# First three hgrn projections taken two chunks of K at a time with the first conditions; norms and transposes ahead of the conditions

## The chip, the cores and the metric

The kernel runs on one core of a Trainium2 chip. The metric is the device time of one execution in microseconds (us); lower is better. The engines are TensorE (PE, with its weight loads shown as PEld), VectorE (DVE), ScalarE (ACT), GpSimd (POOL) and SyncE (SP, which issues the DMAs). All times on rows count from the start of the profiled span.

## The reference

The reference is two transformer blocks in float32 on 256 latent tokens and, in the first block's first layer, 256 context tokens, with width 1024. What matters here is the very beginning of the first block:

```python
m_lat = (silu(c) @ ada_w[0] + ada_b[0])[:, None]        # and the same with c_ctx
sh1, sc1, g1, sh2, sc2, g2 = split(m_lat, 6)
h_lat = rmsnorm(x, norm_g[0, 0]) * (1.0 + sc1) + sh1     # and the same for ctx
z = h @ ab_w_in[0]            # columns: pool 512 | q 512 | zf 512 | zb 512 | v 512 | g 512
q = silu(q); f = lb + (1 - lb) * sigmoid(z_dir); k = 1 - f   # zf forward, zb backward
# gated scan over the tokens for four heads of 128, both directions, then
# output norm, gate, output projection, feed-forward layers, the second layer, the second block
```

`lb` comes from a softmax over `hg_lower`. The first scale `sc1` and shift `sh1` (here: the conditions) need 2 x 1024 columns of `ada_w`, which is 8 MB, before any product with `h` can be made.

## The kernel before

A Python tracer writes the instructions down; a planner in the library then decides each engine's order from the program order and from when operands would be ready, and buffers with the same tag take turns in a fixed number of slots (`bufs`). `issue_after(e)` makes what is traced inside it on e's engine come behind `e` on that engine.

Every large product is split in three: each float32 operand becomes `hi` (ACT, L149) and `lo` (DVE, L150), and `mm3` (L172) makes three matmuls hi·hi, hi·lo and lo·hi into one PSUM tile. A piece of weights goes by DMA into `raw` (four buffers of 512 KB, L161) and is split from there. PSUM has eight banks: three with the tag A, two B, two tr and one C.

The prologue stands in `block1` (L1574) and its helpers. Token tiles 2 and 3 are the context, 0 and 1 the latent. `setup` loads `c` and `c_ctx` and makes `cvec`; the four tiles of x come in; then `ada_first` (L571) returns `step` and `columns`. `step(g)`, g = 0 to 3, loads four buffers `adaw` of 512 KB (L589), multiplies them with `cvec` (sixteen matmuls for each of scale and shift, counted as the profile counts them, L591), adds the bias by one more (L592) and copies the result to `first` (DVE, L595). `columns(g)` turns two chunks of 128 features into columns (L602) and writes `sc` and `sh` (L603 to L605). `modulate(g)` makes h for the same two chunks, scaled and shifted and split into `xh` and `xl`.

The order in the program is: `step(0)`; `gains()`, which loads six small sets of rows by SP's queue (L298) and transposes them; then for each stream its two tiles through `normed` (L642: two Squares on ACT, a power on POOL by L268, scaling on DVE and ACT; its result `u` lives in `big`, two buffers) and sixteen transposes (L237) with copies back over x (L1608); then for g = 1 to 5 the `step(g)`, `columns(g-1)`, `modulate(g-1)` and `products(g-2)`. `products` makes only the first of the three projections of the first two heads, q, two chunks of K at a time: twelve matmuls of 512 columns. The other two, zf and zb, are made in `hgrn_mixer` (L696), `project(0)`, parts 1 and 2, each over all eight chunks at once; part 2 does the context stream first, as 96 matmuls of 256 columns. Behind each part stand a sigmoid (ACT, L745), F and B on DVE (L751, L752) and a product with q on POOL (L759).

Then `levels` (L762) builds the scan in seven levels, a chain over POOL, ACT, PE and DVE (L767 to L807). Beside it PE has two projections of 512 columns for all four tiles (`kept` and `gated`, L866 and L867, 96 matmuls of 512 columns each) and the matmuls of further conditions (`fill`, L529, eight at a time). `outputs(0)` follows (L823 to L848), then `project(1)` and so on.

Of the kernel before, what the change touches and what calls it, by code (L numbers as in the profile page):

```python
# [17 lines left out]
P = 128  # L18
D = 1024
# [62 lines left out]
class Kern:  # L82
# [89 lines left out]
    def mm3(self, ps, lh, ll, rh, rl, first, last):  # L172
        for i, (l, r) in enumerate(((lh, rh), (lh, rl), (ll, rh))):
            self.T.matmul(ps, l, r, start=first and i == 0, stop=last and i == 2)  # L174
            next(self.aside, None)

# [57 lines left out]
    def transposes(self, ps, src, blocks):  # L234

        for i, b in enumerate(blocks):
            self.T.transpose(ps[:, i], src[:, b * P:(b + 1) * P], self.ident)  # L237
# [7 lines left out]

    def new_xT(self):
        self.place = 1 - self.place
        return self.xh[:, self.place], self.xl[:, self.place]
# [42 lines left out]
    def columns(self, rows, name, pool=None):  # L291
# [211 lines left out]
    def gains(self):  # L503
# [8 lines left out]
            (d["pool_scale"].rearrange("o (g p) -> (o g) p", p=P), 4)], "colsA")  # L512
# [58 lines left out]
    def ada_first(self):  # L571
# [5 lines left out]
        every = self.t(self.aw, [P, 2], "every")  # L577
        V.reduce_sum(every, self.ident.rearrange("p (j n) -> p n j", n=32)[:, 0:2], axis=AX.X)
        bias = self.t(self.aw, [24, 256], "bias")
        self.dma(bias, self.d["ada_b"][0].rearrange("(p n) -> p n", p=24))  # L580
        rows = {}

        def step(g):
            ps = self.ps((P, 2, 256))
            for v in (1, 0):

                for h in range(2):
                    raw = self.t(self.aw, [P, 1024], "adaw", bufs=4).rearrange("p (k n) -> p k n", k=4)
                    self.dma(raw, w[:, 4 * h:4 * h + 4, v * 1024 + g * 256:v * 1024 + g * 256 + 256])  # L589
                    for j in range(4):  # L590
                        T.matmul(ps[32 * j:32 * j + 32, v], self.cvec[:, 4 * h + j], raw[:, j], start=h == 0, stop=h == 1 and j != 0)  # L591
                end = T.matmul(ps[0:32, v], self.ident[:24, 4 * v + g:4 * v + g + 1].to_broadcast([24, 32]), bias,  # L592
                               start=False, stop=True)
            rows[g] = self.t(self.aw, [P, 2, 256], "first", bufs=1)
            return end.ins, V.tensor_copy(rows[g], ps).ins  # L595

        def columns(g):
            k = slice(2 * g, 2 * g + 2)
            pc = self.ps((P, 2, 2, 2), "C")
            for v in (1, 0):  # L600
                for c in range(2):
                    T.matmul(pc[:, v, c], rows[g][:, v, c * P:(c + 1) * P], every, start=True, stop=True)  # L602
# [4 lines left out]
        return step, columns, sc, sh  # L607
# [34 lines left out]
    def normed(self, x):  # L642
# [9 lines left out]
        S.activation(u[:, 512:D], x[:, 512:D], AF.Copy, scale=r)  # L652
# [43 lines left out]
    def hgrn_mixer(self, xT, q0, fill):  # L696
# [3 lines left out]
        with self.scope("hg") as hp:  # L700

            mx = self.t(hp, [P, 8], "lbm")
            V.tensor_max(mx, self.hgl[:, 0], self.hgl[:, 1])
            e = self.t(hp, [P, 2, 8], "lbe")
# [1121 lines left out]
```

## Time and profile before

| | us |
|---|---|
| median of 3 runs | 2154.99 (2154.59 to 2156.27) |
| the profiled execution, its own time | 2158.11 |
| its span in the trace | 2156.3 |
| PE busy in the span | 2093.5 (97%) |

The span is what the rows cover; 1.8 us of the profiled execution's time lie outside it, and it is 3.1 us above the median. A busy PE is not always a PE at its peak: a matmul counts from its start to the modelled end, and those in a row overlap. So the pace of PE is read from the starts of its matmuls and from the granted clock.

### The profile page before, as it was taken

Reading aid. Unit: us, or ns where it says so; the run is one execution under the profiler, and the core shown is the slowest. Engines: PE = TensorE matmul, PEld = TensorE weight load, DVE = VectorE, ACT = ScalarE, POOL = GpSimd, SP = SyncE. Lnnn points to the kernel's source line nnn. Section 1 sums busy time; section 2 is a strip of 40 time slices with the busy share of each in tenths; the row PEclk is TensorE's granted clock in tenths of the full one; section 3 lists DMA queues with packets and bytes.
Section 4 is the critical chain, followed back from the end, with each engine's and each line's share of the span. In section 5 each row is a group of like instructions: output and inputs, shape, how many; then the busy total and the mean of one; then the engine's idle time right before and its main releaser. Section 6 shows DMA issues by size and latency. Waiting matters only on the chain. (4 is left out here: it accounts for less than half of the span.)

```text
span 2156.3 us, 33891 instructions
## 1 busy us (share of the span) xinstructions
PE 2093.5 (97%) x13178; PEld 1819.7 (84%) x13178; DVE 1365.8 (63%) x2496; ACT 970.5 (45%) x1904; POOL 160.0 (7%) x182
## 2 busy tenths in 40 slices
PE   7999999999999889999999989999999999999998
PEld 4787878787887668998998878998899889889987
DVE  4656658856535887554754677554855498876556
ACT  4232444322324555543644485543644265355443
POOL 0423200000000210000000000000000012110000
PEclk9999999999999999999999999999999999999999
DMA  9632327767432414655766527655666465137653
GB/s 318 209 125 79 108 74 238 226 207 232 137 102 65 144 38 150 204 181 171 219 180 187 179 75 220 205 181 175 190 205 183 156 167 148 50 110 226 189 184 104
DMA packets 238941, 352.58 MB, mean 164 GB/s; under 512 B 14432, under 2 KB 185020, under 8 KB 238652
## 3 DMA queue, kind: packets, MB, share of 16 engines
q1 hardware_dynamic: 238780, 350.41, 52.2%
q8 instruction: 104, 1.70, 0.3%
q14 instruction: 57, 0.47, 0.1%
HBM read 349.31 MB, written 1.05 MB: 162 GB/s over the span
## 5 line engine op out<-in xcount | busy, mean ns | idle before, releaser
L150 DVE TENSOR_TENSOR lo<-raw,hi 128x512 fp32r<-128x512 f32 (+1 forms) x1072 | 696.3, 692 | 381.2 <-ACT hi L149 379.8
L149 ACT ACTIVATE hi<-raw 128x512 fp32r<-128x512 f32 (+1 forms) x1072 | 601.9, 617 | 740.1 <-issue 356.6
L174 PE MATMUL B<-xh,hi 128*128 128x256 f32 (+1 forms) x1200 | 366.8, 306 | 1.6 <-ACT r L1137 1.4
L174 PE MATMUL B<-xl,hi 128*128 128x256 f32 (+1 forms) x1200 | 366.2, 305 | 1.0 <-DVE xl L150 1.0
L174 PE MATMUL B<-xh,lo 128*128 128x256 f32 (+1 forms) x1200 | 366.6, 306 | 0.0
L174 PE MATMUL A<-xh,hi 128*128 128x256 f32 (+1 forms) x1008 | 304.6, 302 | 0.4 <-ACT a L1383 0.2
L174 PE MATMUL A<-xh,lo 128*128 128x256 f32 (+1 forms) x1008 | 303.5, 302 | 0.7 <-DVE lo L150 0.7
L174 PE MATMUL A<-xl,hi 128*128 128x256 f32 (+1 forms) x1008 | 303.6, 301 | 0.0
L174 PEld LDWEIGHTS B<-xh,hi 128*128 128x128 f32 x1200 | 229.5, 191 | 12.1 <-ACT r L1137 1.6
L174 PEld LDWEIGHTS B<-xl,hi 128*128 128x128 f32 x1200 | 229.6, 191 | 11.3 <-DVE xl L150 1.9
L174 PEld LDWEIGHTS B<-xh,lo 128*128 128x128 f32 x1200 | 229.6, 191 | 10.2 <-issue 1.2
L174 PEld LDWEIGHTS A<-xh,hi 128*128 128x128 f32 x1008 | 193.5, 192 | 8.9 <-ACT hi L149 2.0
L174 PEld LDWEIGHTS A<-xh,lo 128*128 128x128 f32 x1008 | 193.5, 192 | 8.4 <-DVE lo L150 2.0
L174 PEld LDWEIGHTS A<-xl,hi 128*128 128x128 f32 x1008 | 193.6, 192 | 6.1
L174 PE MATMUL B<-hi,xh 128*128 128x512 f32 (+1 forms) x464 | 169.0, 365 | 3.0 <-ACT v L974 1.6
L174 PE MATMUL B<-lo,xh 128*128 128x512 f32 (+1 forms) x464 | 166.9, 360 | 0.0
L174 PE MATMUL B<-hi,xl 128*128 128x512 f32 (+1 forms) x464 | 166.5, 360 | 0.0
L268 POOL TENSOR_TENSOR pow<-rv,mhalf 128x1 f32<-128x1 f32 (+2 forms) x54 | 42.8, 793 | 1441.6 <-DVE rv L273 744.6
L174 PE MATMUL B<-hi,hl 128*128 128x512 f32 x308 | 122.1, 396 | 0.0
L174 PE MATMUL A<-lo,hh 128*128 128x512 f32 x308 | 121.9, 396 | 0.1
L174 PE MATMUL A<-hi,hl 128*128 128x512 f32 x308 | 121.9, 396 | 0.0
L174 PE MATMUL A<-hi,hh 128*128 128x512 f32 x308 | 121.8, 395 | 0.0
(438 smaller groups left out, 3267.5 us busy)
## 6 DMA issues: line engine op xcount, KB each, us to landing
adaw<-in_ada_w SPq DMA_DIRECT2D x96, 512.0 KB, 4.8
raw<-in_ffn_wg SPq DMA_DIRECT2D x88, 512.0 KB, 4.7
raw<-in_ffn_wu SPq DMA_DIRECT2D x88, 512.0 KB, 4.7
raw<-in_ffn_wd SPq DMA_DIRECT2D x88, 512.0 KB, 4.1
raw<-in_ffn_w_in SPq DMA_DIRECT2D x88, 256.0 KB, 4.2
raw<-in_ffn_w_in SPq DMA_DIRECT2D x44, 512.0 KB, 4.5
raw<-in_ab_w_in SPq DMA_DIRECT2D x38, 512.0 KB, 4.6
raw<-in_ffn_w_out SPq DMA_DIRECT2D x38, 512.0 KB, 4.6
```

The source lines that it names most:

```text
L149: self.S.activation(hi, src, AF.Copy)
L150: self.V.tensor_tensor(lo, src, hi.bitcast(F32), op=ALU.subtract)
L174: self.T.matmul(ps, l, r, start=first and i == 0, stop=last and i == 2)
L268: self.G.tensor_tensor(r, x, exponent_tile[:, :x.shape[1]], op=ALU.pow)
```

## The change

It touches only what runs up to the end of the first two heads' projections, and the loads behind them.

- `gains()` and the bias of the conditions are loaded by ACT's queue instead of SP's.
- A new function `first_products` holds the prologue. The adaw loads are issued ahead of the steps, in two sets of four buffers that take turns; the weights of all three projections are loaded and split in halves of K into tiles of their own (48 KB a partition).
- All norms and transposes come first. Every later block of PE's work is chained behind the one before it by `issue_after`: `step(g)`, the q product of group g-1, `columns(g)`, `modulate(g)`, the zf and zb products of group g-1. Last come all three products of group 3. So the six PSUM tiles of the three projections are open at once (two B, three A, one tr), and the steps share one bank of tr.
- `hgrn_mixer` gets the three finished projections; `project(0)` only does what stands behind them. The softmax for `lb` moves to `forget()`, its Exp behind the last norm on ACT.
- The splits of `kept`'s weights on ACT come behind the last sigmoid of `project(0)`.

```diff
@@ gains, columns
-                self.dma(t[at:at + r, :], ap)
+                (dma or self.dma)(t[at:at + r, :], ap)
...
+            (d["pool_scale"].rearrange("o (g p) -> (o g) p", p=P), 4)], "colsA", dma=self.nc.scalar.dma_start)
@@ ada_first
-        self.dma(bias, self.d["ada_b"][0].rearrange("(p n) -> p n", p=24))
-        rows = {}
+        self.nc.scalar.dma_start(bias, self.d["ada_b"][0].rearrange("(p n) -> p n", p=24))
+        ps = self.pst((P, 2, 256))
+        rows, raws = {}, {}
+
+        def load(g):
+            for v in (1, 0):
+                for h in range(2):
+                    raw = self.t(pool if g % 2 else self.aw, [P, 1024], "adaw", bufs=4).rearrange("p (k n) -> p k n", k=4)
+                    raws[g, v, h] = raw
+                    self.dma(raw, w[:, 4 * h:4 * h + 4, v * 1024 + g * 256:v * 1024 + g * 256 + 256])
@@ hgrn_mixer
-                    given = pr == part == 0
-                    if not given:
+                    if pr:
                         wh, wl = self.piece([P, 8, 256], lambda r: [(r, wv[:, :, c0 + 512 * part:c0 + 512 * part + 256])])
...
-                    ps = q0 if given else [self.ps((P, 2, 256), "B") for _ in range(2)]
+                    ps = [self.ps((P, 2, 256), "B") for _ in range(2)] if pr else given[part]
...
-                            for kc in range(0 if given else 8):
+                            for kc in range(8 if pr else 0):
...
-            self.tok_major(self.tiles_of(xT), order, self.wcols(w, 2048, 512), 512, kept, "B")
+            with self.tc.issue_after(hg0_end):
+                pcs = self.wcols(w, 2048, 512)
+            self.tok_major(self.tiles_of(xT), order, pcs, 512, kept, "B")
@@ new
+    def first_products(self, pool, xs):
...
+        load, step, columns, sc, sh = self.ada_first(pool)
+        wv = self.d["ab_w_in"][0].rearrange("(k p) f -> p k f", p=P)
+        w = [[self.t(pool, [P, 8, 256], f"{n}{i}", F32R) for n in ("hi", "lo")] for i in range(3)]
+
+        def weights(h):
+            own = slice(4 * h, 4 * h + 4)
+            for i, (hi, lo) in enumerate(w):
+                raw = self.t(self.w, [P, 4, 256], "raw", bufs=2 * self.nraw)
+                self.dma(raw, wv[:, own, 512 + 512 * i:768 + 512 * i])
+                for k in (0, 2):
+                    self.split(hi[:, 4 * h + k:4 * h + k + 2], lo[:, 4 * h + k:4 * h + k + 2], raw[:, k:k + 2])
+
+        load(0)
+        self.gains()
+
+        for s in (1, 0):
+            uu = [self.normed(xs[2 * s + t]) for t in range(2)]
+            for t, u in enumerate(uu):
+                for c0 in range(0, 8, 4):
+                    ps = self.pst((P, 4, P))
+                    end = self.transposes(ps, u, range(c0, c0 + 4))
...
+        with self.tc.issue_after(self.last):
+            self.lb = self.forget()
...
+        acc = [[self.ps((P, 2, 256), tag) for tag in tags] for tags in ("BB", "AA", ("A", "tr"))]
+
+        def products(g, parts):
+            for i in parts:
+                hi, lo = w[i]
+                for h in range(2):
+                    cut = slice(h * P, (h + 1) * P)
+                    for k in (2 * g, 2 * g + 1):
+                        end = self.mm3(acc[i][h], hi[:, k, cut], lo[:, k, cut], self.xh[:, :, k], self.xl[:, :, k], k == 0, k == 7)
+            return end
...
+        for g in range(4):
+            if g == 0:
+                weights(0)
+                load(1)
+            elif g < 3:
+                load(g + 1)
+            if g == 1:
+                weights(1)
+            for f in (lambda: step(g), lambda: g and products(g - 1, (0,)), lambda: columns(g),
+                      lambda: modulate(g), lambda: g and products(g - 1, (1, 2))):
+                with self.tc.issue_after(end):
+                    end = f() or end
+        with self.tc.issue_after(end):
+            end = products(3, range(3))
+        return acc
```

## Rows read from the trace of the kernel before

**Rows 1.** The page: busy time, share of the span and instructions by engine.

```profile
PE 2093.5 (97%) x13178; PEld 1819.7 (84%) x13178; DVE 1365.8 (63%) x2496; ACT 970.5 (45%) x1904; POOL 160.0 (7%) x182
```

**Rows 2.** Windows: stretch, length, busy by engine (instructions), granted clock, DMA share, GB/s.

```profile
20.10:33.00 12.90, 11.17 (x101) 5.42 (x100) 9.13 (x24) 7.41 (x16) 1.10 (x2) 1.00 0.95 325
33.00:37.50 4.50, 4.50 (x18) 3.67 (x17) 3.50 (x10) 1.75 (x4) 0.00 (x0) 0.64 1.03 332
37.50:54.00 16.50, 15.24 (x94) 10.04 (x92) 9.33 (x22) 8.99 (x16) 0.00 (x0) 1.00 1.07 342
54.00:76.60 22.60, 22.60 (x144) 20.42 (x145) 12.13 (x19) 6.84 (x14) 5.89 (x4) 1.00 0.46 142
76.60:88.00 11.40, 9.69 (x78) 7.37 (x77) 8.97 (x11) 4.90 (x8) 7.46 (x7) 0.85 0.77 241
88.00:150.00 62.00, 61.77 (x357) 47.49 (x356) 33.57 (x55) 17.33 (x30) 21.70 (x30) 1.00 0.47 151
```

**Rows 3.** Timeline, PE and DVE, first condition: start, length, engine, line, tiles, count [idle].

```profile
10.73 1.08 PE L591 MATMUL A<-adaw,cvec 128*32 128x256 f32 x8 [6.02 <-DMA adaw<-in_ada_w]
...
13.98 1.94 PE L591 MATMUL A<-adaw,cvec 128*32 128x256 f32 x16
...
16.84 0.34 PE L301 MATMUL tr<-ident,rows 52*128 52x52 f32 x1
16.94 0.69 DVE L595 COPY first<-A 128x512 f32<-128x512 f32 x1 [7.35 <-PE A L592]
```

**Rows 4.** Timeline, ACT, Silu and norms of the first two tiles.

```profile
4.00 0.31 ACT L496 ACTIVATE rows<-rows 16x128 f32<-16x128 f32 x1
...
5.25 0.63 ACT L649 ACTIVATE big<-r 128x512 f32<-128x512 f32 x1 [0.94 <-DMA r<-in_ctx]
...
9.11 0.72 ACT L652 ACTIVATE big<-r,pow 128x512 f32<-128x512 f32 x1 [0.49 <-POOL pow L268]
```

**Rows 5.** Tile rows: issues by line, duration ns min/median/max, first and last start.

```profile
L298 SPq DMA_DIRECT2D rows<-in_norm_g x4: 287/296/1920, 7.4 to 10.1; - x4
```

**Rows 6.** Timeline, PE: transposes early and later.

```profile
17.11 3.08 PE L237 MATMUL tr<-ident,big 128*128 128x128 f32 x12
...
26.41 0.63 PE L237 MATMUL tr<-ident,big 128*128 128x128 f32 x4 [0.73 <-DVE big L651]
```

**Rows 7.** Timeline, PE: last condition, columns, and the products behind them.

```profile
38.62 1.07 PE L591 MATMUL A<-adaw,cvec 128*32 128x256 f32 x16
...
41.71 1.05 PE L602 MATMUL C<-every,first 128*128 128x2 f32 x8
...
42.63 0.48 PE L174 MATMUL B<-xh,hi 128*128 128x512 f32 x1
```

**Rows 8.** Timeline: from the first columns to the first product.

```profile
28.57 0.95 PE L602 MATMUL C<-every,first 128*128 128x2 f32 x8
...
34.10 0.65 PE L174 MATMUL B<-xh,hi 128*128 128x512 f32 x1
```

**Rows 9.** Timeline, all engines, where the projections end.

```profile
71.13 0.38 ACT L745 ACTIVATE sg<-B 128x256 f32<-128x256 f32 x1 [1.42 <-PE B L174]
...
72.62 1.40 POOL L759 TENSOR_TENSOR A<-q,F 128x512 f32<-128x512 f32 x1 [2.68 <-DVE F L751]
...
76.61 1.05 PE L772 MATMUL A<-q,ks 128*128 128x128 f32 x8
...
77.60 1.93 PE L529 MATMUL C<-adaw,cvec 128*32 128x256 f32 x32
...
79.81 3.60 DVE L150 TENSOR_TENSOR lo<-raw,hi 128x512 fp32r<-128x512 f32 x3
...
81.67 1.77 PE L772 MATMUL A<-q,ks 128*128 128x128 f32 x8 [1.71 <-POOL ks L767]
```

**Rows 10.** Timeline: last step of the levels, first transpose of the outputs.

```profile
117.44 0.18 DVE L807 TENSOR_TENSOR F<-F 128x8 f32<-128x8 f32 x1
...
150.33 0.60 PE L823 MATMUL tr<-ident,B 128*128 128x128 f32 x4
```

More of the change, by code (lines that the diff above doesn't have):

```diff
@@ L173, in mm3 @@
         for i, (l, r) in enumerate(((lh, rh), (lh, rl), (ll, rh))):
-            self.T.matmul(ps, l, r, start=first and i == 0, stop=last and i == 2)
+            m = self.T.matmul(ps, l, r, start=first and i == 0, stop=last and i == 2)
             next(self.aside, None)
+        return m.ins
     @contextlib.contextmanager
@@ L289, in bcast, with columns @@
         return t
-    def columns(self, rows, name, pool=None):
+    def columns(self, rows, name, pool=None, dma=None):
         n = sum(r for _, r in rows)
@@ L601, in columns @@
                 for c in range(2):
-                    T.matmul(pc[:, v, c], rows[g][:, v, c * P:(c + 1) * P], every, start=True, stop=True)
+                    end = T.matmul(pc[:, v, c], rows[g][:, v, c * P:(c + 1) * P], every, start=True, stop=True)
             V.tensor_scalar(sc[:, k], pc[:, 1], 1.0, 32.0, op0=ALU.add, op1=ALU.mult)
@@ L605, in columns @@
             V.tensor_copy(sh[:, k], pc[:, 0])
-        return step, columns, sc, sh
+            return end.ins
+        return load, step, columns, sc, sh
     def ada_cols(self, l, v):
@@ L693, in post_end, with hgrn_mixer @@
             self.V.scalar_tensor_tensor(out[:, sl], self.post_y[tl, h], r, x[:, sl], op0=ALU.mult, op1=ALU.add)
[L696 removed]
+    def hgrn_mixer(self, xT, given, fill):
         d, V, S, G, T = self.d, self.V, self.S, self.G, self.T
@@ L1595, in block1 @@
                 self.dma(xs[tl], xin[tl])
-            step, columns, sc, sh = self.ada_first()
-            step(0)
-            self.gains()
-            wv = d["ab_w_in"][0].rearrange("(k p) f -> p k f", p=P)
-            for s in (1, 0):
-                uu = [self.normed(xs[2 * s + t]) for t in range(2)]
-                for t, u in enumerate(uu):
-                    for c0 in range(0, 8, 4):
-                        ps = self.pst((P, 4, P))
-                        self.transposes(ps, u, range(c0, c0 + 4))
-                        self.V.tensor_copy(xs[2 * s + c0 // 4].rearrange("p (c n) -> p c n", n=256)[:, :, t * P:(t + 1) * P], ps)
@@ L1631, in block1 @@
-            for g in range(1, 6):
-                with contextlib.ExitStack() as after:
-                    if g < 4:
-                        for e in step(g):
-                            after.enter_context(self.tc.issue_after(e))
-                    if g < 5:
-                        columns(g - 1)
-                        modulate(g - 1)
-                    if g == 1:
-                        piece = self.piece([P, 8, 256], lambda r: [(r, wv[:, :, 512:768])])
-                    if g > 1:
-                        products(g - 2)
@@ L1643, in block1 @@
-            cat = self.hgrn_mixer(xT, q0, self.ada(0, (2, 4, 3)))
+            with self.scope("start") as start:
+                given = self.first_products(start, xs)
+            xT = [self.halves(i) for i in range(2)]
+            cat = self.hgrn_mixer(xT, given, self.ada(0, (2, 4, 3)))
             first.close()
```

91 lines of the change are left out of this document (47 added, 44 removed).

## The prediction

> **What bounds the kernel now.** I read the page first: PE is busy for 2093.5 us of the span, far more than any other engine [rows 1]. So a gain is either less work on PE or less of its time lost. The change leaves PE's work as it is: the same step, column, transpose and product matmuls, in another order. It can only win back time that PE loses in the stretch it touches. Second I read the windows of that stretch, to see where PE is short of its pace [rows 2]. From 54.0 to 76.6 it is busy all the time, with 144 matmuls for the last two projections (48 of 512 columns, 96 of half that): 22.6 us, 11.3 a projection. So 2.8 us is the price of one projection's two chunks, and 8.5 of all three. Ahead of that PE sits idle 1.7 us between 20.1 and 33, 1.3 between 37.5 and 54, and from 33 to 37.5 its granted clock reads 0.64, part of it at the lower of its two levels, about 1.6 us lost. Behind it, from 76.6 to 88, there are 1.7 us idle and a clock of 0.85, another 1.7. From 88 on PE is as good as full [rows 2], and the chain of the seven levels ends at 117.4 while kept and gated last to 150.3 [rows 10]; that chain has 33 us of slack and sets nothing. So the time at which PE is through the three projections, 76.6, and what it loses just after, decide the result; what follows moves along with them.
>
> Third I read the timeline of the first 17 us. PE starts on the first condition at 10.73, when its weights land, and is through it at 16.84, where the rows' transpose stands; all of this lies under the loads and beside the norms [rows 3]. The sixteen matmuls of one vector take 1.94 us there and 1.07 us later [rows 3, 7], and four transposes take a third of 3.08, 1.03 us, against 0.63 [rows 6]: PE is at its lower pace up to about 20 us, though the granted clock column doesn't show it.
>
> **Part by part.**
>
> *Norms and transposes first.* This is the part that costs. Silu ends at 4.31 and the first Square starts at 5.25 as its tile lands [rows 4]. The six small loads of gains now stand on ACT between the two, since their buffer is free only after Silu. Each issue takes 0.30 us by the median and 1.92 at most on SP's queue [rows 5]; none is on ACT in this trace. Six make 1.8 us by the median, so the Squares start at 6.1 (5.25 if they are put behind the Squares, 15.8 if each takes the maximum). I take 6.1, the row's median being that of a free queue, and ACT's own is free. From the first Square to the second tile's scaled result it is 4.6 us (5.25 to 9.83) [rows 4]. The first tile is scaled some 1.2 us before that; its eight transposes take 2.05 at the lower pace, the second tile's as much, and since u has two buffers the next pair can only follow its transposes. That gives 3.4 + 2.05 + 0.2 for the first tile, 2.05 for the second, then 3.2 for the last tile's own chain and 2.05 for its transposes: 13.0 us from the first Square, so the transposes end at 19.1. At the higher pace it would be about 12.
>
> *The first condition behind them.* Its loads have long landed, yet it waits on PE's order to 19.1. At the pace of 13.98 it takes 5.6 us, at the later one 3.1 (38.62 to 41.71, both vectors with their biases) [rows 3, 7]. I take 4.4, since PE is at its lower pace till then and speeds up after a stretch of steady work: 23.5. The copy of 0.69 us is no longer covered [rows 3], 0.8 with its hand-over; the columns take 0.9 (41.71 to 42.63) [rows 7], with half of the lower pace 1.2. So 25.5. From the end of the first columns (29.52) to the first product (34.10) it is 4.6 us [rows 8]; the second step's 3.1 lies inside. The first product starts at 30.1.
>
> *The chained order from there.* PE has four times 8.5 of products, two more steps of 3.1 and three more columns of 0.9: 42.9 us without a wait, for a copy lies under a q product of 2.8, and a modulation of 4.6 under 5.6 of zf and zb products and a step of 3.1. The projections end at 30.1 + 42.9 = 73.0, against 76.6: **3.6 us earlier**. Per part: 1.7 and 1.3 of idle time and 1.6 of low clock go away, and the two uncovered waits and the late first step come in.
>
> *Loads.* Two MB of x, 8 of adaw and 3 of weights make 13 MB, at the 325 to 342 GB/s of the stretch [rows 2] 38 to 40 us; the last condition's weights land near 41 and are used after 50. The second condition's land near 24, before 26. A second set of adaw buffers takes away waits on SP's queue, which cost nothing at this rate. SP's queue loses seven short issues, and adaw moves up by about 2 us. Behind adaw the fill's loads and kept's weights come in order while PE is full. All this I cost at zero; the cover is PE's 42.9 us.
>
> *Behind the projections.* Part 2 used to end one stream 5.6 us before the other, so that the first levels' matmuls stood ready at 76.61 [rows 9]. Now all of part 2 ends within the last 2.8 us. After the last matmul there are three sigmoids of 0.38 [rows 9], then the first `hi` of kept, held behind them by the added wait, then its `lo` on DVE. DVE makes three `lo` in 3.60 us there while POOL works [rows 9], 1.2 each; ACT takes 0.63 for as many elements [rows 4]. With 1.1 of sigmoids, 0.6 of `hi`, 1.2 of `lo` and 0.4 of hand-overs the first `lo` is there at 3.3. Queued behind that wait on ACT are kept's splits alone; PE waits for them. PE has the four loaded slices of the next conditions, 1.93 us [rows 9], then it idles about 1.4 us until that `lo`, and may starve by 0.5 us for each of three more. Before, the same place lost 1.71 idle [rows 9] and the 1.7 of clock. So between 3.4 saved and 3 lost: I take 1.5 lost, because the levels' first product now comes some 5.6 us behind the projections (a last product of 1.40 on POOL [rows 9] with another still queued ahead of it, the sum of keys, about as long, and 1.4 of sigmoid and hand-overs) and before it was ready.
>
> *What has one answer.* `forget` moves seven tiny operations and a table load from one idle place to another, zero; the open PSUM tiles are free there, zero; the code after `project(0)` is the same.
>
> The sum: 3.6 - 1.5 = 2.1 us less. The profiled execution's 2158.1 becomes 2156.0 (span 2154.2); the median of runs, 3.1 below it, **2152.9**.
>
> **A rule weighed.** The rows show PE slow through its first steps and the transposes at 17.11, and fast from about 20. The Trainium skill, TensorE: Matmul & The Clock Gate, Part 4 on the PE-mode transpose, says that transposes don't count as work that lifts PE's clock. By it the first condition and its columns would run wholly at the lower pace; the trace can't tell, because steps and transposes alternate in it.
>
> **Rivals.**
>
> 1. *The early stretch is short.* The loads of gains cost ACT nothing and PE is at its higher pace from the middle of the transposes. Then they end at 5.25 + 12 = 17.2, the step takes 3.1, and the projections end at 17.2 + 3.1 + 0.8 + 0.9 + 4.6 + 42.9 = 69.5, 7.1 us earlier. With nothing lost behind them it is 2147.9, with the 3.4 of before saved too 2144.5. For it: the tiles land by 5.25 and the norms wait for nothing else. Against it: the pace in [rows 3, 6].
>
> 2. *PE stays at its lower pace through the first condition and the columns.* By [rows 3, 7] that is 1.2 us more for the step and 0.6 for the columns: 1.8 less gain, 2154.7, no change. By the rule of the Trainium skill above (TensorE: Matmul & The Clock Gate, Part 4) it would be this one.
>
> 3. *The gain is given back behind the projections.* PE waits for the levels' first sum of keys, 5.6 us, with 1.93 of slices and little of kept beside: 3.6 lost, 2155.0. For it: kept's splits now stand behind the sigmoids on ACT, F and B on DVE. Against it: the slices and the first `lo` need no levels.
>
> 4. *Slower: ACT's issues hold back the norms.* The place is ACT between Silu and the first Square, and everything on PE is chained behind the last transposes. At 1.92 us an issue the Squares start at 15.8 in place of 6.1, the projections end at 82.7, and with 1.5 behind them it is 2155.0 + 6.1 + 1.5 = 2162.6. It decides from about 1.4 us an issue on, where the loss passes 0.2%. For it: the maximum in [rows 5], while big loads were in issue, as they will be. Against it: the median.
>
> **How the numbers follow.** Forecast 0.43, rival 1 0.27, rival 2 0.10, rival 3 0.08, rival 4 0.12. A measurement of this kernel can tell about 0.2%, 4.3 us, from no change: faster is below 2150.7, slower above 2159.3. The forecast's own range is 2150 to 2156: up to 3 us more from a quick first step and nothing lost behind, as much less from the opposite. All of rival 1 and a little of the forecast are faster: 0.29. Rival 4 is slower, and at smaller prices of an issue the same: 0.11. The rest, 0.60, is no change. The range reaches to most of rival 1 and to the mild half of rival 4: 2147 to 2159.5.
>
> **What would show it.** Right, step by step: all 32 transposes ahead of the first step, ending at 18 to 20; the first Square near 6; the first product near 30; no PE idle over 0.3 us from there to the projections' end near 73; then an idle of 1 to 3 us until kept's splits. Wrong: transposes ending after 23 (rival 4) or before 17.5 (rival 1), idle time of PE between the groups (a load or a modulation that is late), or PE below its pace after 30 us.

## The result, and the profile after

The changed kernel takes 2169.81 us (median of 4 runs, 2167.31 to 2171.87) against 2155.63 for the kernel before in the same runs: ratio 1.0058, 95% interval 1.0043 to 1.0074. It is slower by 0.58%, about 12.5 us by the ratio (the two medians are 14.2 us apart), and lies above the predicted range of 2147 to 2159.5. The profiled execution, the shortest of the four at 2167.31 us, spans 2165.5 us in its trace, 9.2 more than before.

On the page of the changed kernel PE's work is the same as in [rows 1] (busy time, share, instructions):

```profile
PE 2092.8 (97%) x13130; PEld 1817.9 (84%) x13130; DVE 1366.4 (63%) x2496; ACT 970.8 (45%) x1904; POOL 160.7 (7%) x182
```

So 9.2 us of idle time and pace were lost. Two milestones tell where: the end of the three projections moves from 76.6 to 80.9, 4.3 us later and not 3.6 earlier; the first transpose of the outputs moves from 150.33 [rows 10] to 160.00, 9.7 later:

```profile
160.00 0.60 PE L822 MATMUL tr<-ident,B 128*128 128x128 f32 x4
```

Behind that the two traces agree to 0.5 us. So 4.3 us come ahead of the projections' end and 5.4 behind it.

The windows of the changed kernel (stretch, length, busy by engine PE, PEld, DVE, ACT, POOL with instructions, granted clock, DMA share, GB/s) answer to [rows 2]:

```profile
22.40:36.40 14.00, 13.22 (x82) 4.81 (x81) 7.68 (x19) 4.90 (x10) 0.00 (x0) 1.00 1.09 348
36.40:39.50 3.10, 3.10 (x8) 2.47 (x8) 0.69 (x1) 0.00 (x0) 0.00 (x0) 1.00 1.10 348
54.00:80.80 26.80, 26.80 (x143) 20.03 (x143) 7.31 (x18) 7.84 (x13) 0.00 (x0) 1.00 0.31 108
80.80:88.20 7.40, 2.07 (x33) 0.94 (x32) 7.39 (x11) 4.54 (x10) 5.83 (x5) 0.95 0.69 211
88.20:95.00 6.80, 6.46 (x26) 5.22 (x26) 6.36 (x8) 2.60 (x4) 5.78 (x5) 0.55 0.79 255
```

From 39.5 to 80.8 PE is full, as foreseen (14.50 of 14.50 us up to 54.0, then the third row). The hole is 80.8 to 88.2: DVE is busy all the time there and PE for 2.07 of 7.40 us; after it the granted clock is 0.55 for 6.8 us, about 3.1 us lost. The idle time and the lower clock of these two stretches, less the 3.4 us that the place cost before, account for the 5.4 behind the projections to within 0.5 us. And from 22.4 to 36.4 PE is busy 13.2 of 14 us with work that was counted at 8.7 (4.4 + 1.2 + 3.1).

The timeline of PE over that stretch (start, length, engine, line, tiles, count, idle before) shows why:

```profile
11.35 1.97 PE L238 MATMUL tr<-ident,big 128*128 128x128 f32 x8
...
20.42 1.98 PE L238 MATMUL tr<-ident,big 128*128 128x128 f32 x8 [1.29 <-DVE big L664]
22.34 1.94 PE L602 MATMUL tr<-adaw,cvec 128*32 128x256 f32 x16
...
28.89 1.87 PE L614 MATMUL C<-every,first 128*128 128x2 f32 x8 [0.78 <-DVE first L606]
30.69 1.93 PE L602 MATMUL tr<-adaw,cvec 128*32 128x256 f32 x16
...
36.39 0.80 PE L174 MATMUL B<-xh,hi 128*128 128x512 f32 x1
...
36.98 0.63 PE L174 MATMUL B<-xl,hi 128*128 128x512 f32 x1
37.41 0.63 PE L174 MATMUL B<-xh,lo 128*128 128x512 f32 x1
...
40.09 0.40 PE L174 MATMUL B<-xh,hi 128*128 128x512 f32 x1
40.33 0.40 PE L174 MATMUL B<-xl,hi 128*128 128x512 f32 x1
```

The transposes come in four runs of eight with a wait of 0.6 to 1.3 us between them and end at 22.4. Both steps take, for sixteen matmuls, the 1.94 us that [rows 3] show, not the 1.07 of [rows 7]; the first products stand 0.43 us apart, those from 40 on 0.23 to 0.24. So PE is at its lower pace until 39.5, though the granted clock reads 1.00.

ACT's timeline, with its queue's issues (ACTq), has the start of it:

```profile
5.54 0.63 ACT L662 ACTIVATE big<-r 128x512 f32<-128x512 f32 x1 [1.33 <-DMA r<-in_ctx]
5.54 0.63 ACTq L303 DMA_DIRECT2D rows<-in_norm_g  x2
...
6.20 0.66 ACTq L303 DMA_DIRECT2D rows<-in_norm_g  x2
6.89 0.34 ACTq L303 DMA_DIRECT2D rows<-in_hg_lower  x1
8.08 0.25 ACTq L303 DMA_DIRECT2D rows<-in_pool_scale  x1
8.38 0.63 ACT L662 ACTIVATE big<-r 128x512 f32<-128x512 f32 x1 [2.13 <-DMA r<-in_x]
```

The first two of the six loads are issued beside the first Square of the first tile and the other four between its two Squares, 6.2 to 8.3, at 0.25 to 0.34 us each with one pause of 0.85. The row names a load of x as what ended the second Square's wait; the experiment with gains behind the norms, below, shows that it was the issues.

Behind the projections, all engines:

```profile
80.93 1.93 PE L534 MATMUL C<-adaw,cvec 128*32 128x256 f32 x32
...
81.15 0.86 DVE L750 TENSOR_SCALAR F<-sg,omlb,lb 128x512 f32<-128x512 f32 x2
...
81.82 4.40 POOL L758 TENSOR_TENSOR A<-q,F 128x512 f32<-128x512 f32 x3 [62.07 <-PE C L534]
...
82.47 2.63 DVE L750 TENSOR_SCALAR F<-sg,omlb,lb 128x256 f32<-128x256 f32 x2
...
83.86 0.38 ACT L744 ACTIVATE sg<-tr 128x256 f32<-128x256 f32 x1 [1.41 <-DVE F L750]
84.14 3.21 ACT L149 ACTIVATE hi<-raw 128x512 fp32r<-128x512 f32 x6
...
87.88 0.68 DVE L150 TENSOR_TENSOR lo<-raw,hi 128x512 fp32r<-128x512 f32 x1
...
88.21 1.06 PE L534 MATMUL C<-adaw,cvec 128*32 128x256 f32 x2 [5.35 <-DMA adaw<-in_ada_w]
...
96.96 0.50 PE L174 MATMUL B<-hi,xh 128*128 128x512 f32 x1
```

The last sigmoid starts at 83.86, since its buffer waits for an F of DVE; beside POOL's product F takes three times as long as one of twice the size just before; so kept's splits start at 84.14 on ACT and its first `lo` at 87.88 on DVE. PE has four slices of the next conditions (a slice is eight matmuls on one loaded buffer), then idles 5.35 us. By the row, it waits for a fifth slice, whose weights land at 88.2 and which the planner put ahead of all else. But kept's first `lo` is through only at 88.56, and the levels' first sum of keys (`ks`) at 87.81, so three waits end there together. The fifth slice moves with the projections' end and stands at no fixed time: SP's queue waits 27.5 us, until the last product, with the load of `c_pairs`, and issues the slice's load at 81.70; in all experiments on the changed kernel the slice lands 7.0 to 7.5 us behind the first of the four.

### The profile page after: what moved, and what is told of

It reads as the page before. It is cut to its first block, busy times and chain, and to the rows that moved or that the text cites. A ratio compares the mean times of both kernels' runs of the same rounds, so it can differ in the third digit from the quotient of the medians.

```text
span 2165.5 us, 33790 instructions
## 1 busy us (share of the span) xinstructions
PE 2092.8 (97%) x13130; PEld 1817.9 (84%) x13130; DVE 1366.4 (63%) x2496; ACT 970.8 (45%) x1904; POOL 160.7 (7%) x182
## 5 line engine op out<-in xcount | busy, mean ns | idle before, releaser
L174 PE MATMUL B<-xh,hi 128*128 128x256 f32 (+1 forms) x1152 | 351.7, 305 | 1.4 <-ACT r L1139 1.4
L174 PE MATMUL B<-xh,lo 128*128 128x256 f32 (+1 forms) x1152 | 351.0, 305 | 0.0
L174 PE MATMUL B<-xl,hi 128*128 128x256 f32 (+1 forms) x1152 | 350.3, 304 | 0.0
L174 PE MATMUL A<-xh,hi 128*128 128x256 f32 (+1 forms) x1032 | 313.5, 304 | 0.5 <-ACT a L1385 0.3
L174 PE MATMUL A<-xh,lo 128*128 128x256 f32 (+1 forms) x1032 | 312.0, 303 | 1.8 <-DVE lo L150 1.8
L174 PE MATMUL A<-xl,hi 128*128 128x256 f32 (+1 forms) x1032 | 312.3, 303 | 0.0
L174 PEld LDWEIGHTS B<-xh,hi 128*128 128x128 f32 x1152 | 220.5, 191 | 12.1 <-issue 2.4
L174 PEld LDWEIGHTS B<-xh,lo 128*128 128x128 f32 x1152 | 220.5, 191 | 9.6 <-issue 1.2
L174 PEld LDWEIGHTS B<-xl,hi 128*128 128x128 f32 x1152 | 220.6, 192 | 8.6 <-issue 0.5
L174 PE MATMUL B<-hi,hh 128*128 128x512 f32 x308 | 121.8, 395 | 0.0
```

Source lines behind the costliest of these rows:

```text
L174: m = self.T.matmul(ps, l, r, start=first and i == 0, stop=last and i == 2)
```

## The experiments

Times of the kernel before are those of the runs beside each experiment; all ratios go by them. Three milestones, times read from the traces, are given for each: the first product, the end of the projections (the first matmul behind them) and the first transpose of the outputs. They are 34.1, 76.6 and 150.3 in the kernel before, 36.4, 80.9 and 160.0 in the changed one.

### Gains and bias by SP's queue

```diff
-            ..., "colsA", dma=self.nc.scalar.dma_start)
+            ..., "colsA")
-        self.nc.scalar.dma_start(bias, ...)
+        self.dma(bias, ...)
```

> The changed kernel with the loads of gains and of the bias back on SP's queue. In the changed kernel ACT issues six of them between its first Square at 5.54 and its second at 8.38, where 0.63 would do. Theory A (these issues hold the norms back): the transposes end at 20.2 in place of 22.4, the three projections at 78.6 in place of 80.8, the time is about 2 us less, 2167.5. Rival B (the norms' own chain over ACT, DVE and POOL sets the end of the transposes): they end at 22 or later, the time stays within 1 us of 2169.8.

Ratio 1.0060 (1.0040 to 1.0081); milestones 35.8, 78.8, 157.7. On SP the six rows come behind adaw, and their transpose on PE stands ahead of all others:

```profile
16.54 0.32 PE L306 MATMUL tr<-ident,rows 52*128 52x52 f32 x1 [11.95 <-DMA rows<-in_hg_lower]
16.78 3.93 PE L238 MATMUL tr<-ident,big 128*128 128x128 f32 x16
23.19 1.94 PE L238 MATMUL tr<-ident,big 128*128 128x128 f32 x8 [2.47 <-DVE rv L671]
25.52 1.97 PE L238 MATMUL tr<-ident,big 128*128 128x128 f32 x8 [0.39 <-DVE r L1620]
27.42 1.39 PE L602 MATMUL tr<-adaw,cvec 128*32 128x256 f32 x16
...
29.28 1.07 PE L602 MATMUL tr<-adaw,cvec 128*32 128x256 f32 x16
```

So it doesn't measure the issues and tests neither theory: the transposes end 5.1 us later than in the changed kernel. It shows something else. The first condition goes over to the higher pace within its first sixteen matmuls, and the rest stays there; that more than pays for the delay, and the first product comes 0.6 us earlier. What stood ahead were sixteen transposes without a wait and, 2.47 us later, sixteen more with one of 0.39.

### The first condition free among the transposes

```diff
         load(0)
+        step(0)
         self.gains()
...
-            for f in (lambda: step(g), lambda: g and products(g - 1, (0,)), ...
+            for f in (lambda: g and step(g), lambda: g and products(g - 1, (0,)), ...
```

The step takes an A bank, as in the kernel before.

> The changed kernel with the first condition's matmuls free to run among the transposes, as before the change, in a PSUM bank of tag A. Theory A (the first condition waits on PE's order while PE idles between the transposes): its 5.8 us and the copy behind it go from the path, the columns start near 23 in place of 28.9, the projections end at 74 to 76 in place of 80.8, the time is 5 to 7 us less, 2163 to 2165. Rival B (PE is at its lower pace until full-size products have run, wherever the condition stands): the columns come earlier by as much, but the lower pace lasts as long behind them and 3 us or more of it come back: projections end at 77 or later.

Ratio 1.0032 (1.0017 to 1.0046); milestones 31.1, 76.6, 155.5. The projections end 4.3 us earlier than in the changed kernel, just as in the kernel before: the uncovered step was worth what was lost up to there. But the first product comes only at 31.1 and at the lower pace, since the second step, which starts at the higher pace at 24.6, now waits for its weights (1.16 and 0.79 us), and PE falls back within it; from 30 to 35 the granted clock reads 0.50, the lower of its two levels (1.2 of 2.4 GHz).

### Kept's splits not held back

```diff
-            with self.tc.issue_after(hg0_end):
-                pcs = self.wcols(w, 2048, 512)
+            pcs = self.wcols(w, 2048, 512)
```

> The changed kernel without the order that keeps the splits of kept's weights on ACT behind the last sigmoid. In the changed kernel PE idles 5.35 us from 82.9 to 88.2 and makes kept's first matmul at 97.0. Theory A (the held-back splits, first lo at 87.9, leave PE nothing to do there): the first matmul of kept comes within 3 us of the projections' end, the idle falls under 1 us, the clock stays up, and the outputs start 6 to 8 us earlier, near 153; time 2162 to 2164. Rival B (PE's order holds a slice of the next conditions ahead of kept, and that slice's load lands at 88.2 whatever the splits do): the idle of 5 us stays and the time is within 1.5 us of 2169.8.

Ratio 1.0006 (0.9990 to 1.0022); milestones 36.9, 81.1, 154.3. PE, behind the projections:

```profile
82.99 0.50 PE L174 MATMUL B<-hi,xh 128*128 128x512 f32 x1
...
88.23 0.64 PE L534 MATMUL C<-adaw,cvec 128*32 128x256 f32 x8 [0.88 <-DMA adaw<-in_ada_w]
```

Everything up to 81 is as in the changed kernel; behind it kept starts at 82.99 and not at 96.96, and 5.7 us are won. The fifth slice still lands at 88.2. PE now has kept's matmuls up to there, and the planner puts them ahead of it. So the slice was not the cause, nor were the levels, whose first matmul comes at 89.83 here: the held splits were. The one line `issue_after(hg0_end)` is the largest single loss of those undone one by one (4.5 at the outputs in the second experiment).

### Two matmuls of the identity behind each tile's transposes

```diff
                     end = self.transposes(ps, u, range(c0, c0 + 4))
+                    if c0:
+                        with self.tc.issue_after(end):
+                            end = extra(2)    # 128x128, ident by ident
```

> The changed kernel with two more matmuls of the identity by itself (128 columns, result unused) behind each tile's sixteen transposes' second half, in time in which PE idles between the norms. The output doesn't change. Theory A (the gaps between the transposes keep PE at its lower pace, 1.94 us for sixteen matmuls of a condition up to 36 us): with the gaps filled the pace rises before the first condition, which takes nearer 3.1 than 5.8, and the projections end 3 to 6 us earlier, 75 to 78. Rival B (the conditions' own matmuls bring the pace down or leave it low, whatever ran before): the first two conditions take 5.8 each as now, and the projections end at 80.8 or up to 1 us later.

Ratio 1.0042 (1.0023 to 1.0060); milestones 32.7, 78.5, 157.6. (The profile counts each of these float32 matmuls twice, so two show as x4.) Of PE's waits between the transposes the first is gone; the other two, 1.21 and 1.26 us, stay. The pace rises all the same, within the second tile's transposes (1.48 us for eight, then 1.06), and the first condition takes 3.1 us (21.85 to 24.9) in place of 5.8. But its copy then leaves PE idle for 1.75, the second step is slow again from about 29, and products are 0.43 apart until 39. Of the 3.7 us that the first product wins, 2.4 are left at the projections' end. Theory A has the time of the first condition right, though only one wait was filled; the second step is slow as rival B said, but only behind a wait.

### Two edits: condition free, splits not held back

The edits of the second and the third experiment together.

> The first condition stands free among the transposes and kept's splits are not held back; the rest is the changed kernel. Theory (the two losses are separate places, so their gains add): the projections end near 76.5 us as with the first edit alone (80.8 in the changed kernel), the idle of PE behind them is below 2 us, the outputs' first transpose starts near 150 (160.0 in the changed kernel, 155.5 and 154.3 with one edit each), ratio to the kernel before 0.998 to 1.001. Rival (they don't add: with PE earlier the loads behind the projections, on SP's queue in order, set the place): PE again idles 4 us or more there, outputs near 154, ratio 1.0005 to 1.003.

Ratio 1.0002 (0.9991 to 1.0013); milestones 31.4, 77.3, 150.5. The gains add: 9.5 us at the outputs, against 4.5 and 5.7 singly, and PE idles 0.78 at the fifth slice. The kernel is as fast as the one before and no faster: PE now waits 2.49 us for the first modulation and makes the first products at the lower pace again.

### The two edits, with the wait ahead of the second step filled

```diff
-                      lambda: modulate(g), lambda: g and products(g - 1, (1, 2))):
+                      lambda: None if g else extra(12), lambda: modulate(g), lambda: g and products(g - 1, (1, 2))):
```

and the two matmuls behind each tile's transposes, as above.

> As the kernel with two edits, with 20 added matmuls of the identity whose result nobody reads: two behind each tile's transposes and twelve between the first columns and the second step, where PE otherwise waits for loads. Theory (the low pace from 27 to 36 follows the stretch in which PE has only conditions and waits): with that stretch filled the second step takes about 3.1 us and not 5.7, the products start at the higher pace (0.23 to 0.24 us apart from the first on), the projections end near 73.5, the outputs' first transpose starts near 147, ratio 0.996 to 0.999. Rival (the low pace comes from the conditions themselves, whatever stands beside them): the second step is slow again, products 0.43 apart, and the added matmuls only cost their 2 to 4 us: projections end at 77 to 79, outputs 150 to 152, ratio 1.000 to 1.002.

Ratio 1.0013 (1.0004 to 1.0022); milestones 37.3, 80.3, 152.9. The filling was badly placed: it writes PSUM's one C bank, which is free only when DVE has read the columns, and DVE has six `lo` in its order ahead of that. DVE, then PE:

```profile
26.25 2.49 DVE L150 TENSOR_TENSOR lo<-raw,hi 128x512 fp32r<-128x512 f32 x4
28.66 0.15 DVE L618 TENSOR_SCALAR sc<-C 128x4 f32<-128x4 f32 x1
```

```profile
29.03 5.20 PE L1616 MATMUL C<-ident 128*128 128x128 f32 x24 [3.28 <-DVE sc L619]
34.16 1.07 PE L605 MATMUL tr<-adaw,cvec 128*32 128x256 f32 x16
```

The time is the one that the rival gave, but not for its reason: the milestones are later than it said, and the step and the products are not slow. Two things follow. Behind the 24 matmuls (at the lower pace, 0.22 us each) the whole second step and all products go at the higher pace: the conditions don't bring the lower pace by themselves. And the columns' reading, which sets the first modulation, waits for weight splits that nobody needs yet.

### Gains by ACT, behind the norms

```diff
-        self.gains()
...
         with self.tc.issue_after(self.last):
+            self.gains()
             self.lb = self.forget()
```

> The changed kernel with the six loads of gains issued by ACT behind the norms and not between the Squares. Theory (the issues on ACT hold back the norms by 2.2 us): the second Square follows the first at once, near 6.2 us and not at 8.4, the 32 transposes end at 20 to 20.3 (22.4 in the changed kernel), and the projections end 2.2 us earlier, near 78.6; with the idle behind them as it is, outputs near 157.8, ratio 1.0045 to 1.005. Rival (the norms come tile by tile and their powers and copies set the pace, not the issues): transposes still end after 21.5, ratio about 1.0058. Second rival (the loads, now late, come in behind those of adaw): PE sits idle at the rows' transpose before the first step, which starts after 22.

Ratio 1.0052 (1.0040 to 1.0064); milestones 33.1, 78.6, 157.5. ACT, then PE:

```profile
5.86 0.61 ACT L662 ACTIVATE big<-r 128x512 f32<-128x512 f32 x1
```

```profile
19.96 0.23 PE L306 MATMUL tr<-ident,rows 52*128 52x52 f32 x1 [1.66 <-DMA rows<-in_pool_scale]
20.13 1.07 PE L602 MATMUL tr<-adaw,cvec 128*32 128x256 f32 x16
...
21.85 1.94 PE L602 MATMUL tr<-adaw,cvec 128*32 128x256 f32 x16
```

The second Square follows at once, and the transposes end at 18.3, 4.1 us earlier: more than the 2.2 of the issues, as the planner now makes the norms in pairs (two runs of sixteen transposes, 3.92 and 3.75 us, 2.09 apart). 1.7 of it go to the wait for the rows, so that step and projections come 2.2 and 2.4 us earlier, as the first theory said and in part by the second rival's way. The pace is the higher one for one vector of the condition and falls in the second.

### Three edits

The two edits, and gains behind the norms.

> The kernel with two edits (first condition free among the transposes, kept's splits not held back), and gains loaded by ACT behind the norms. Theory (with the first condition among the transposes it is the landing of the second condition's weights near 25.8 us that sets the second step, so what the norms win is lost again): projections end within 0.7 us of the kernel with two edits (about 76.5), ratio 0.998 to 1.001. Rival (the norms set it): the projections end 2 us earlier, near 74.5, outputs near 148, ratio 0.997 to 0.9995.

Ratio 1.0004 (0.9995 to 1.0014); milestones 31.1, 75.9, 149.0. The columns come at 19.9 in place of 24.2, yet the first product moves by 0.3 us only: the second step waits 2.61 us for `sc` on DVE, behind the same `lo`, and then for its weights. The time is that of the two edits, as the theory said; of the 2 us that the rival gave, 1.5 show at the projections' end.

### All that was found, with eight matmuls of the identity

```diff
-                weights(0)
+                wload(0, (0,))
                 load(1)
+                wload(0, (1, 2))
+                wsplit(0, (0,))
...
+            if g == 1:
+                plan = (lambda: products(0, (0,)), lambda: step(1), lambda: products(0, (1,)), lambda: columns(1),
+                        lambda: modulate(1), lambda: products(0, (2,)))
...
+            if g < 2:
+                with self.tc.issue_after(self.behind), self.tc.issue_after(self.behind_s):
+                    wsplit(g, range(1 - g, 3))
```

All this comes on top of the three edits. `behind` and `behind_s` are the last `lo` and `hi` of the modulation. Eight matmuls of the identity stand behind the first columns and the rows' transpose.

> On top of the kernel with three edits (first condition among the transposes, kept's splits not held back, gains behind the norms): the weights of zf and zb are split only behind the first modulation, so that VectorE's six lo of 0.64 us no longer stand ahead of the first scale; the second condition's weights are loaded ahead of those of zf and zb; the first q products stand ahead of the second step; and eight matmuls of the identity, whose result nobody reads, fill PE's wait for the first modulation. Theory (all that was found adds up): first product near 25 us (31.1 in the kernel with three edits), PE at its higher pace within 2 us of it, projections end at 71 to 72.5 (75.9), outputs' first transpose at 144.5 to 146 (149.0; 150.3 in the kernel before), ratio 0.997 to 0.9985. Rival (what is won early is waited for at the loads, which come at 348 GB/s whatever PE does: 13 MB take until about 41 us and the last half of the weights is late): PE idles between the groups, projections end after 74.5, ratio 0.999 to 1.0005.

Ratio 0.9990 (0.9978 to 1.0002); milestones 26.4, 74.5, 148.8. The first product is 4.7 us earlier, the projections only 1.4. PE idles 3.15 us ahead of the products and makes them at the lower pace; ACT, which they wait for, loads the table for the Exp of `lb` in between its two halves of the modulation (0.60 us at 22.57, 0.58 at 25.13). The rival's time is met, but not by its loads: from the first product to the projections' end PE waits for none.

```profile
23.19 1.28 ACT L1588 ACT_TABLE_LOAD   x1
```

```profile
26.42 0.73 PE L174 MATMUL B<-xh,hi 128*128 128x512 f32 x2 [3.15 <-ACT xh L149]
...
28.17 0.63 PE L174 MATMUL B<-xh,hi 128*128 128x512 f32 x1
28.59 0.63 PE L174 MATMUL B<-xl,hi 128*128 128x512 f32 x1
```

### The same without the eight matmuls

```diff
-                plan = lambda: columns(0), lambda: extra(), lambda: modulate(0)
+                plan = lambda: columns(0), lambda: modulate(0)
```

> The same without the eight matmuls of the identity. Theory (PE's lower pace follows the wait for the first modulation, and products at the lower pace stand 0.43 us apart against 0.23): the first product comes at the same time, near 25 us, but the first 12 to 24 products go at the lower pace, 2.4 to 4.8 us lost, projections end at 73.5 to 76, ratio 0.9985 to 1.000. Rival (the products lift the pace themselves within 2 us, or the wait is too short to lower it): projections end within 1 us of the kernel with the added matmuls.

Ratio 0.9995 (0.9985 to 1.0005); milestones 26.6, 74.7, 147.7. The rival has the number, for another reason than its two: with an idle of 5.45 us ahead of the products or 3.15 the pace is the lower one, and it rises at 30 in both, 3.5 to 4 us after the first product. Filling only a part of the wait is worth nothing.

### The kernel before, with kept's splits held back

```diff
-            self.tok_major(self.tiles_of(xT), order, self.wcols(w, 2048, 512), 512, kept, "B")
+            with self.tc.issue_after(hg0_end):
+                pcs = self.wcols(w, 2048, 512)
+            self.tok_major(self.tiles_of(xT), order, pcs, 512, kept, "B")
```

> The kernel before with one part of the change alone: kept's splits on ACT stand behind the last sigmoid of the first two heads. Theory (the hold costs only where all sigmoids and all F and B come together at the end): here the last sigmoid is at 77.2 us and the first hi at 76.7, so kept's first lo moves from 77.4 to about 78.5 to 80, its first matmul by no more than 2 us, and PE has the slices beside it: outputs within 1 us of 150.3, ratio 0.9998 to 1.0008. Rival (the hold is a loss by itself): outputs at 152 to 155, ratio 1.001 to 1.002.

Ratio 1.0029 (1.0016 to 1.0041); projections end 76.3, outputs 152.2. The rival is right, the hold is a loss by itself. The sigmoids end here as early as foreseen, but with the splits behind them the planner deals kept's `lo` out among the levels' steps on DVE, and the first matmul of kept moves from 79.46 to 85.83, though its first `lo` moves by 0.8 us only:

```profile
85.83 0.50 PE L174 MATMUL B<-hi,xh 128*128 128x512 f32 x1
```

### All edits, with the softmax behind the second modulation

```diff
-            self.lb = self.forget()
...
                 with self.tc.issue_after(self.behind), self.tc.issue_after(self.behind_s):
+                    if g:
+                        self.lb = self.forget()
                     wsplit(g, range(1 - g, 3))
```

> The kernel with all edits and the eight added matmuls of the identity (result unread), with the softmax for lb moved behind the second modulation, so that ACT's table load of 1.28 us and the Exp no longer stand between the two halves of the first modulation. Theory (the first product waits for ACT's modulation, and with 1.5 us less of it the added matmuls reach nearly up to the first product, so that PE keeps its higher pace): first product near 24.9 us (26.4), the first twelve products 0.23 to 0.3 us apart and not 0.43, second step from 28 (31.2), projections end at 71 to 72 (74.4), outputs' first transpose at 145.5 to 147 (148.8), ratio 0.9970 to 0.9985. Rival (an idle of even 1.5 us before the products lowers the pace, as it did after 3): products 0.43 apart again, projections end at 72.5 to 73.5, ratio 0.9982 to 0.9995. Second rival (earlier projections only lengthen the wait for the fifth slice behind them, whose load comes in SP's order): projections end early, but outputs stay within 1 us of 148.8.

Ratio 0.9976 (0.9963 to 0.9989); median 2155.19 against 2160.61 beside it; milestones 25.2, 71.9, 146.1.

```profile
21.34 3.30 PE L1646 MATMUL A<-ident 128*128 128x128 f32 x16
25.23 0.76 PE L174 MATMUL B<-xh,hi 128*128 128x512 f32 x2 [0.59 <-ACT xh L149]
26.04 0.50 PE L174 MATMUL B<-xl,hi 128*128 128x512 f32 x1
26.38 0.39 PE L174 MATMUL B<-xh,lo 128*128 128x512 f32 x1
...
71.89 1.93 PE L534 MATMUL C<-adaw,cvec 128*32 128x256 f32 x32
78.99 0.64 PE L534 MATMUL C<-adaw,cvec 128*32 128x256 f32 x8 [2.00 <-DMA adaw<-in_ada_w]
```

With an idle of only 0.59 us in front of them the products are at the higher pace from the second on, and the projections end 4.7 us earlier than in the kernel before. This version is faster than both kernels, by 0.24% than the kernel before; the wait of 2.00 for the fifth slice is left in it. The theory holds at every milestone. The first rival, a wait of 1.5 us, did not come about; the second is wrong, since the slice comes earlier too (78.99 against 88.21 in the changed kernel).

## Why the prediction was wrong

The sum put the outputs at 150.3 - 2.1 = 148.2; they came at 160.0. The 11.8 us between are 7.9 at the projections' end and 3.9 behind it.

*Norms and transposes first: too small by 3.3 us.* The price of an issue was right (0.25 to 0.34 us), the place was not: they hold back the second Square by 2.2 us, where the sum had the first one 0.85 later, and the planner then made the norms tile by tile, so that PE waits between the runs of transposes. Without them (gains behind the norms) the transposes end at 18.3, 13.1 us behind the first Square, which is the sum's own 13.0. That is next to rival 4's place, with a price of 2.2 us on the path (4.1 on the transposes) and not its 1.92 an issue. One term was missing altogether: the gains themselves, whose rows must be transposed on PE ahead of the first transposes of x or of the first step.

*The first condition and the columns: too small by 2.0.* 5.8 for 4.4, and 2.6 with the copy for 2.0. I took half of the lower pace because PE was to speed up after a stretch of steady work. That step failed: PE was busy 13.2 of 14 us with the two conditions and stayed at its lower pace all through them. This is rival 2, and the pace stayed low beyond what that rival said: the second step cost 1.1 more up to the first product, and eight products 1.4 more. The terms sum to 7.8.

*A rule weighed.* Rival 2's outcome came about, but the rule does not carry it. In the first experiment the pace rose right behind two runs of sixteen transposes. With gains behind the norms it rose too, where PE had done nothing but transposes (the condition behind them took 1.07 us for sixteen matmuls). By the Trainium skill, TensorE: Matmul & The Clock Gate, Part 4, transposes don't count as work that lifts the clock. These two traces don't agree with that, and the measurement decides. What differs in the changed kernel is that its transposes come in runs of eight with a wait behind each; in the fourth experiment, where matmuls of the identity joined the first two runs, the pace rose as well. Why the conditions' own 14 us did not lift it stays open.

*The chained order from there: right.* 42.9 us without a wait were foreseen; 36.4 to 80.9 is 44.5, 1.4 of it the lower pace at its start. No load and no modulation was late in that stretch of the changed kernel. They become late as soon as the front is faster (two edits, three edits), which the forecast, with loads at zero, could not say.

*Behind the projections: too small by 3.9.* The first `lo` of kept was to be through 3.3 us behind the projections' end; it starts 7.0 behind it and is through at 7.6. Two things failed. The sigmoids were counted as 1.1 us on ACT; they share two buffers, each free only when DVE has made its F. And F and B were not in the sum: they stand on DVE ahead of the `lo`, beside POOL's products, where an F of 256 columns takes 1.3 us and more. Named as queued behind the wait was ACT's work alone; DVE's queue and the planner's answer to the wait were what cost. The experiment on the kernel before shows that the hold loses even where the sigmoids are early. Rival 3 named the loss of this place, but by the levels; that it was not they that decided is shown by the third experiment: with the splits free PE had kept's work at once. The loads behind the projections, put at nothing, also end there (the fifth slice), but by the same experiment they did not decide either.

The profile's signs that were named did tell: transposes ending at 22.4, near the 23 of rival 4, and PE below its pace after 30 us.

*Open.* By their ratios, the timed runs of all kernels with held splits lose more than their traces show at the outputs (the changed kernel 12.5 us against 9.7; gains behind the norms 11.2 against 7.1; the kernel before with the hold 6.3 against 1.8); those without lie to either side (two edits 0.4 against 0.2; the last one -5.2 against -4.2; kept's splits free alone 1.3 against 4.0; three edits 0.9 against -1.3). The intervals reach 2 to 4 us to either side, and a trace is one execution: that of kept's splits free took 2167.18, 7.5 above its median. Behind the outputs this trace and that of the kernel before with the hold show a granted clock of 0.98 from 1250 to 1350 us and 0.95 from 1750 to 1850, where the kernel before shows 1.00 and 0.97. The mean granted clock of the timed runs is 0.987 to 0.993 in the kernels with held splits, 0.992 to 0.995 in those without and 0.994 to 0.995 in the kernel before. Why it should be lower with the hold stays open.

## What to carry to other kernels

Work on PE that used to fill the waits of the transposes was not free to move behind them: its price was its whole time, at PE's lower pace, and here the pace stayed low for the 14 us of conditions and beyond. A wait that is put on one engine's splits must be costed on every engine that the splits pass, here DVE with F, B and `lo`, and with the order that the planner makes of it: in the kernel before, the hold moved kept's first `lo` by 0.8 us and its first matmul by 6.4. Moving the front of a chain pays only up to the next thing that was hidden (here, one by one: the gains' rows, DVE's unneeded `lo`, the second condition's weights, a table load), so each must be moved before the gain is there.

## What was not expected of the hardware

The granted clock of a window can read 1.00 while the matmuls in it stand at half their pace (22.4 to 39.5 in the changed kernel, 0.43 us apart against 0.23); in the second experiment the same pace is shown as 0.50. The windows read here have a pattern: ahead of the first rise of the pace the lower one reads 1.00, and behind a fall it reads 0.50 to 0.52 (33 to 38 us in the fourth experiment, 22 to 33 with gains behind the norms, 29 to 34 with the wait filled). The spacing of equal matmuls is the surer sign.

Sixty and more condition matmuls in 13.2 busy us of 14, with one wait of 0.78, did not raise PE's pace, while 24 matmuls of the identity in 5.2 us, or two runs of sixteen transposes, stood ahead of a rise; and behind those a whole step kept the higher pace. Behind a wait of 1.66 us (gains behind the norms) the pace fell within the step, behind one of 3.15 the products were at the lower one, behind one of 0.59 not. The length of the wait does not decide alone: behind a wait of 2.00 for the fifth slice (all edits, softmax behind) the pace fell, behind one of 1.93 (without the eight matmuls) it did not.

VectorE made two F of 512 columns in 0.86 us and, beside POOL's products (4.40 us for three, 1.47 each), two of half that size in 2.63, 1.3 each: about as long as one product. The Trainium skill, SBUF — State Buffer, Who interferes with whom, says that VectorE in its two-port modes, which a tensor_scalar may take, and GpSimd lock each other out for a whole instruction. The trace agrees with that, though it doesn't show in which mode F was made.
